# Stick-breaking and retention step: the places of the samples' pages, the last block of a group, and how the prompt's attention output is read

## The chip, the core and the metric

One NeuronCore of a Trainium2 chip runs the whole program. The metric is the device time of one execution in microseconds (us), and the time of a kernel is the median of its runs. The engines are TensorE (PE in the profile; PEld is its loading of weights), VectorE (DVE), ScalarE (ACT), GpSimd (POOL) and SyncE (SP). SP issues most DMAs, POOL issues the indirect ones. Each of them works through its own instructions in a fixed order.

## What is computed

One layer of a decoder, for a prompt of 1024 positions and for 8 samples of 8 new positions with 2048 past positions each. The part that matters here is stick-breaking attention, 8 heads of 64:

```python
def sb_block(q, k, v, q_pos, bias):
    z = jnp.einsum('bqhd,bkhd->bhqk', q, k) * (SB_HEAD_DIM ** -0.5)
    z = z + bias[None, :, None, None]
    mask = jnp.arange(k.shape[1])[None, :] < q_pos[:, None]
    log_stay = jnp.where(mask, jax.nn.log_sigmoid(-z), 0.0)
    tail = lax.cumsum(log_stay, axis=3, reverse=True) - log_stay
    a = jnp.where(mask, jnp.exp(jax.nn.log_sigmoid(z) + tail), 0.0)
    return jnp.einsum('bhqk,bkhd->bqhd', a, v)
...
    m = sigmoid(a_sb) * (o_sb @ w_sb_out) + sigmoid(a_r) * (o_r @ w_ret_out)
    h = h + rms_norm(m @ w_o, g_m_post)
```

The keys and values of a sample's past lie in 16 pages of 128 positions each, in a pool in HBM, in an order that a table gives; a page of keys is 256 KB for all heads, and the kernel reads 512 KB at once. Before and behind the mixer stand two SwiGLU layers that the change doesn't touch.

## The kernel before

`mixer_in` (L1471) makes the mixer's projections, retention, the prompt's attention (`prompt_sb`, L888) and the samples' attention (`decode_sb`, L1070); `mixer_out` (L1510) multiplies what attention gave with w_sb_out, adds the retention branch and multiplies with w_o. A framework arranges the instructions of each engine at compile time: it goes through the program in its order and simulated time and takes what is ready. Tiles lie in pools, pools are laid out as a stack, and a pool that is opened where older ones were closed lies on their bytes. On the chip an instruction waits only for earlier users of its own bytes.

**Fill.** Products that nobody waits for soon (gates and the retention branch's output, 448 steps of `gate_steps` and `ret_steps`) are given out as fill: `through(gen, k)` runs a generator and takes k fill steps for each of its yields. A step is some products of 320 or 384 columns on TensorE (L133, L137, L138). FILL_DEC has the five values of k for decode: one for the logits of group 0, one for each of the pairs (logits of group g + 1, values of group g), one for the values of group 3. 12 steps stand between the prompt's heads and decode. What is left of the fill runs behind decode.

**The prompt's heads.** Each of 8 heads has four tiles of 4 KB a partition, qs, kh, kl and vs, in the pool pqk, with three buffers each: heads 0, 3 and 6 share one, 1, 4 and 7 another, 2 and 5 the third. A head's block goes: two products into PSUM (L1031, L1032), sigmoids on ACT, a copy of the last column (L1047), a scan (L1049) and a product (L1050) on DVE, transposes on TensorE (L999), their high and low parts (L96 on ACT, L99 on DVE), products with vs (L1011), and the output through ost to osT in HBM (L1018, L1019).

**The samples.** Two samples make a group, there are four groups. `logits(g)` has 8 blocks of keys; for one it gathers two tiles of pages (L1100), transposes them in 16 products (L1202) into kt, with two copies each on DVE (L1207) and ACT (L1209), and with one block's lag multiplies kt with the queries qd (`product`, L1115). After every second block the sigmoids (L1149, L1150), the scan (L1156) and the product bt (L1157) follow, and with a further lag bt's transposes (`weights`, L1179, copied at L1180). The last block's product and weights stand at the end of `logits`, one behind the other (L1219 to L1224). `values(g)` gathers pages of values and multiplies them with the weights, from the last block to the first. `both` takes a step of logits and a step of values in turn. Key pages have six buffers and value pages five, in the pool decp, that lies on pqk; the first page tile lies on the qs of heads 0, 3 and 6. The query tile qd, the new keys kn and two kt are in deck; kn and qd lie on the vs of head 7, kt on what follows it. The bias rows brow (L1085, 16 small DMAs), the mask, the result odec and the weights of the new keys atn (L1109, a memset) are in dec, on the prompt's pt, bt and at.

**The end of decode.** The remaining fill runs, odec goes to the last 64 columns of osT (L1275), and `mixer_out` reads osT in three chunks of columns, four tiles each, into raw tiles sq (L1528) of the pool mg, that lies on the mixer's input u; from them come the high parts sh on ACT (L96) and the low parts sl on DVE (L99), in the pool mo, that lies on decode's pools. Products with w_sb_out follow (L1533 to L1548), for which SP loads the gates and the retention branch into the tiles xr (L1542, L1544) of mg.

Of the kernel before, what the change touches and what calls it, by code (L numbers as in the profile page):

```python
# [43 lines left out]
FILL_DEC = (.6, .8, .8, .8, .6)  # L44
# [24 lines left out]
class Trunk:  # L69
# [99 lines left out]
    def setup(self):  # L169
        nc, io = self.nc, self.io  # L170
        self.const = self.pool("const")
        self.wraw = self.pool("wraw")
        self.psum = self.pool("psum", space=PSUM)
        self.dram = self.pool("dram", space=DRAM)
        cp = self.const
        self.ident = self.t(cp, [P, P], "ident")
        make_identity(nc, self.ident)
        self.ones = self.t(cp, [P, P], "ones")
        nc.vector.memset(self.ones, 1.0)
        self.minus_half = self.t(cp, [P, 4], "mhalf")  # L180
        nc.gpsimd.memset(self.minus_half, -0.5)
        self.rowix = self.t(cp, [P, NB * PAGES // 2], "rowix", I32)
        self.gain = {}
        self.xT = self.t(self.dram, [D, T], "xT")
        self.h1T = self.t(self.dram, [D, T], "h1T")
        self.h2T = self.t(self.dram, [D, T], "h2T")
        self.osT = self.t(self.dram, [512, T], "osT")
        self.orT = self.t(self.dram, [D, T], "orT")
        self.gaT = self.t(self.dram, [D, T], "gaT")
        self.gbT = self.t(self.dram, [D, T], "gbT")  # L190
        self.grT = self.t(self.dram, [D, T], "grT")
        self.mrT = self.t(self.dram, [D, T], "mrT")
        self.unT = self.t(self.dram, [D, 512], "unT")
        self.cB = self.t(self.dram, [P, 8, 4, 288], "cB")
# [693 lines left out]
    def prompt_sb(self):  # L888
        nc, io = self.nc, self.io
        win = io["w_in"][0]  # L890
        with ExitStack() as ctx:
            qp = self.pool("pqk", ctx)
# [12 lines left out]
            def proj(p):  # L905

                qs = [self.t(qp, [P, TP], "qs", F32R, bufs=3) for e in range(2)]
                kh = [self.t(qp, [P, TP], "kh", F32R, bufs=3) for e in range(2)]
                kl = [self.t(qp, [P, TP], "kl", F32R, bufs=3) for e in range(2)]
                vs = [self.t(qp, [P, 8, P], "vs", F32R, bufs=3) for e in range(2)]  # L910
# [159 lines left out]
    def decode_sb(self):  # L1070
# [5 lines left out]
        with ExitStack() as ctx:  # L1076
            pp = self.pool("decp", ctx)
            kp_ = self.pool("deck", ctx)
            dp = self.pool("dec", ctx)
# [11 lines left out]
            kn = self.t(kp_, [P, 4, TD], "kn")  # L1091
# [13 lines left out]
            qd = self.t(kp_, [P, 288], "qd")  # L1105
            nc.gpsimd.memset(qd, 0.0)
# [17 lines left out]

            def logits(g, ats):


                qv = qd.rearrange("q (b x) -> q b x", x=144)[:, :, :P].rearrange("q b (m y) -> q b m y", y=32)
# [54 lines left out]
                def product(ps, b2, j, kt):  # L1183
                    side_by_side(ps, partial(query, b2), lambda m: kt[:, m, :], b2 == 0, b2 == 1)
                    if b2:
                        bt = self.t(dp, [P, 512], "bt", bufs=2)
                        left[0] = stick(bt, ps.rearrange("q (h i x) -> q h x i", h=2, i=2), 512, left[0])
                        todo.append((j, bt))

                late, todo, left = [], [], [None]  # L1190
                nk = new_keys()
                step = 0
                for j in range(NG - 1, -1, -1):
                    ps = self.bank("pb")
                    for b2 in range(2):
                        kp = [gather(self.t(pp, [P, 1024], "page", bufs=6), ck, 2 * g + b2, 2 * j + x)
                              for x in range(2)]
                        kt = self.t(kp_, [P, 4, 512], "kt", bufs=2)
                        for m in range(4):
# [10 lines left out]
                            if late and m == 1:  # L1210
                                product(*late.pop(0))
                            if todo and b2 == 1:
                                weights(*todo.pop(0))
# [4 lines left out]
                        late.append((ps, b2, j, kt))  # L1218
                while late:  # L1219
                    product(*late.pop(0))  # L1220
                yield
                while todo:
                    weights(*todo.pop(0))
                yield  # L1224

            def values(g, ats):
                po = self.bank("pm")
                for b2 in range(2):
                    out = po[:, b2 * P : (b2 + 1) * P]
                    for j in range(NG, -1, -1):  # L1230
                        for i in range(4 if j < NG else 1):
                            if j < NG and i % 2 == 0:
                                vp = gather(self.t(pp, [P, 1024], "vpage", bufs=5), cv, 2 * g + b2, 2 * j + i // 2)
# [32 lines left out]
            for g in range(4):  # L1266
                if g < 3:
                    new = {}
                    self.through(both(logits(g + 1, new), values(g, ats)), FILL_DEC[1 + g])
                    ats = new  # L1270
                else:
                    self.through(values(g, ats), FILL_DEC[4])
            while self.tiles or self.live:
                self.fill(1)
            nc.sync.dma_start(self.osT.rearrange("(m q) t -> q m t", q=P)[:, :, TP:T], ost)  # L1275
# [234 lines left out]
    def mixer_out(self):  # L1510
        nc, io = self.nc, self.io
        mch = [(0, 512), (512, 288), (800, 288)]
        with ExitStack() as ctx:
# [6 lines left out]
            with ExitStack() as ctx2:  # L1520
                op = self.pool("mo", ctx2)
                sh, sl = {}, {}
                for c, (o, n) in reversed(list(enumerate(mch))):
                    sh[c], sl[c] = (self.t(op, [P, 4, n], f"s{x}{c}", F32R) for x in "hl")
                for c, (o, n) in enumerate(mch):
                    for q in range(4):
                        raw = self.t(gp, [P, 512], "sq", bufs=4)
                        nc.sync.dma_start(raw[:, :n], self.osT[q * P : (q + 1) * P, o : o + n])  # L1528
                        self.hi(sh[c][:, q, :n], raw[:, :n])
                        self.lo(sl[c][:, q, :n], raw[:, :n], sh[c][:, q, :n])  # L1530
# [303 lines left out]
```

## Time and profile before

| | us |
|---|---|
| median of 3 runs | 2906.24 |
| the runs | 2904.14 to 2907.02 |
| the profiled execution, device time | 2907.92 |
| its span in the profile | 2906.2 |
| mean granted clock of TensorE, share of full speed | 0.986 |

The span is what the profiler recorded of one execution. Head 7 of the prompt ends at about 1658 us of it, decode runs from there to about 1952, and the products with w_sb_out follow. Times on the left of a timeline's rows are us from the start of the span. In a row of the stretches the length of the stretch is followed by the busy time of each engine with the number of its instructions. The granted clock is a share of 2.4 GHz, so that 0.50 is 1.2 GHz. "issue" as a releaser means that the engine waited for nothing that the profile shows.

### The profile page before, as it was taken

What the parts mean: (1) busy time and instruction counts of PE and PEld (TensorE: products, weight loads), DVE (VectorE), ACT (ScalarE), POOL (GpSimd) and SP (SyncE); (2) the same over time, 40 slices, a digit from 0 to 9 for tenths busy, and PEclk for the clock granted to TensorE, in tenths of its full rate; (3) what the DMA queues carried; (4) which work ended last, traced back from release to release, by engine and by line L of the source; (5) the groups of instructions that cost most, each with busy time, mean ns of one, the idle gap of its engine ahead of it and who ended that gap; (6) DMA issues with size and microseconds to landing.
All of it is one profiled execution on the core that took longest, in us unless ns stands there. A gap on an engine that the chain in (4) does not pass through costs nothing.

```text
span 2906.2 us, 51637 instructions
## 1 busy us (share of the span) xinstructions
PE 2804.2 (96%) x20064; PEld 2638.4 (91%) x20064; DVE 2033.5 (70%) x3962; ACT 1221.7 (42%) x2498; POOL 763.1 (26%) x687
## 2 busy tenths in 40 slices
PE   7999999999999999999999889989989999999998
PEld 6998899999999999989999767778988998999998
DVE  7878878888753543546888654436578888788776
ACT  5443444443343333335666542213344444434443
POOL 2334413333150000000000245520024335133321
PEclk8999999999999999999999999999999999999998
DMA  6544443333242322332222389876324335433431
GB/s 168 149 129 130 152 153 123 103 118 108 78 152 88 102 84 85 93 113 79 76 74 76 124 301 321 294 253 192 107 80 127 116 111 180 129 101 106 133 88 42
DMA packets 420420, 380.63 MB, mean 131 GB/s; under 512 B 30352, under 2 KB 380944, under 8 KB 420176
## 3 DMA queue, kind: packets, MB, share of 16 engines
q1 hardware_dynamic: 397904, 306.03, 34.4%
q0 software_dynamic: 22272, 71.31, 7.2%
q8 instruction: 157, 2.57, 0.4%
q14 instruction: 87, 0.71, 0.1%
HBM read 310.03 MB, written 63.05 MB: 128 GB/s over the span
## 4 chain that ended last, share of the span: by engine, by line
PE 59%; DVE 4%; issue 3%; DMA 1%; POOL 1%; ACT 1%; another core or an unknown queue 0%; SPq 0%; POOLq 0%; DVEq 0%; ACTq 0%
PE pa L133 11%; PE pa L138 10%; PE pa L137 10%; PE pb L133 3%; PE pb L138 3%; PE pb L137 3%; PE pc L133 3%; PE pc L137 3%; PE pc L138 3%; PE pc L1202 2%; PE pm L1115 1%; PE pm L1011 1%; PE pc L999 1%; PE pb L1115 1%; DVE sl L99 1%
## 5 line engine op out<-in xcount | busy, mean ns | idle before, releaser
L96 ACT ACTIVATE sh<-wr 128x512 fp32r<-128x512 f32 x592 | 339.2, 622 | 394.3 <-POOL wr L590 161.6
L133 PE MATMUL pa<-uh,wh 128*128 128x384 f32 (+1 forms) x1408 | 477.6, 339 | 4.7 <-ACT qdec L920 2.0
L138 PE MATMUL pa<-uh,wl 128*128 128x384 f32 (+1 forms) x1408 | 465.4, 331 | 0.0
L137 PE MATMUL pa<-ul,wh 128*128 128x384 f32 (+1 forms) x1408 | 464.3, 330 | 0.4 <-POOL ul L99 0.4
L133 PE MATMUL pa<-q,sh 128*128 128x256 f32 (+1 forms) x1408 | 411.7, 292 | 31.8 <-ACT hf L658 15.7
L99 DVE TENSOR_TENSOR sl<-wr,sh 128x512 fp32r<-128x512 f32 x592 | 397.0, 698 | 60.3 <-ACT sh L96 56.6
L137 PE MATMUL pa<-q,sh 128*128 128x256 f32 (+1 forms) x1408 | 409.6, 291 | 1.8 <-DVE q L99 1.8
L138 PE MATMUL pa<-q,sl 128*128 128x256 f32 (+1 forms) x1408 | 408.8, 290 | 0.8 <-DVE sl L99 0.8
L137 PE MATMUL pc<-hl,whd 128*128 128x256 f32 (+2 forms) x1088 | 350.2, 323 | 1.6 <-DVE hl L99 1.6
L138 PE MATMUL pc<-hh,wld 128*128 128x256 f32 (+2 forms) x1088 | 350.1, 323 | 0.0
L133 PE MATMUL pc<-hh,whd 128*128 128x256 f32 (+2 forms) x1088 | 343.4, 324 | 4.4 <-DVE y L718 2.4
L718 DVE TENSOR_TENSOR y<-y,pc 128x256 f32<-128x256 f32 (+2 forms) x496 | 248.8, 515 | 133.6 <-PE pc L138 131.3
L133 PE MATMUL pb<-q,sh 128*128 128x288 f32 (+1 forms) x1088 | 313.8, 289 | 3.3 <-ACT q L96 1.5
L138 PE MATMUL pb<-q,sl 128*128 128x288 f32 (+1 forms) x1088 | 314.5, 289 | 0.4 <-DVE sl L99 0.4
L137 PE MATMUL pb<-q,sh 128*128 128x288 f32 (+1 forms) x1088 | 314.7, 289 | 0.0
L133 PEld LDWEIGHTS pa<-q,sh 128*128 128x128 f32 x1408 | 268.5, 191 | 38.6 <-ACT hf L658 17.6
L133 PEld LDWEIGHTS pa<-uh,wh 128*128 128x128 f32 x1408 | 266.4, 189 | 20.8 <-issue 10.2
L137 PEld LDWEIGHTS pa<-q,sh 128*128 128x128 f32 x1408 | 268.3, 191 | 4.0 <-DVE q L99 2.1
L138 PEld LDWEIGHTS pa<-q,sl 128*128 128x128 f32 x1408 | 267.7, 190 | 2.1 <-DVE sl L99 1.0
L137 PEld LDWEIGHTS pa<-ul,wh 128*128 128x128 f32 x1408 | 266.4, 189 | 3.3 <-issue 1.4
L138 PEld LDWEIGHTS pa<-uh,wl 128*128 128x128 f32 x1408 | 265.8, 189 | 2.8 <-issue 1.7
L588 POOL TENSOR_TENSOR wr<-wr 128x512 f32<-128x512 f32 x78 | 125.7, 1612 | 481.8 <-DVE sl L99 476.7
(340 smaller groups left out, 5962.5 us busy)
## 6 DMA issues: line engine op xcount, KB each, us to landing
wr<-in_w_ffn_gu_dram SPq DMA_DIRECT2D x176, 512.0 KB
wrd<-in_w_ffn_down_dram SPq DMA_DIRECT2D x88, 512.0 KB
wr<-in_w_in_dram SPq DMA_DIRECT2D x56, 512.0 KB
q<-cB SPq DMA_DIRECT2D x16, 576.0 KB
wr<-in_w_o_dram SPq DMA_DIRECT2D x10, 512.0 KB
cB<-y SPq DMA_DIRECT2D x32, 144.0 KB
cB<-xr SPq DMA_DIRECT2D x32, 144.0 KB
s<-in_state_ret_dram SPq DMA_DIRECT2D x16, 256.0 KB
```

The lines of the kernel that those rows point to most:

```text
L96: return self.nc.scalar.activation(dst, src, AF.Copy)
L99: (eng or self.nc.vector).tensor_tensor(dst, src, hi.bitcast(F32), op=ALU.subtract)
L133: ins = mm(ps, wh, xh, start=first, stop=False)
L137: mm(ps, wh, xl, start=False, stop=False)
L138: mm(ps, wl, xh, start=False, stop=last)
L588: tt(v1, v0, v1, op=ALU.add)
L718: nc.vector.tensor_tensor(y[p][:, d, c], y[p][:, d, c], ps[:, :n], op=ALU.add)
L999: nc.tensor.transpose(tp[:, j * P : (j + 1) * P], bt[:, j * P : (j + 1) * P], self.ident)
L1011: ins = nc.tensor.matmul(po[:, lo:256], vs[:, j, :], ats[j // 4][x][:, j % 4, lo:256], start=(j == 0 and x == 0), stop=(j == last and x == 1))
L1115: return nc.tensor.matmul(out[32 * m : 32 * m + 32], w(m), x(m), start=first, stop=last, skip_group_check=True)
L1202: ins = nc.tensor.transpose(tp[:, i * P : (i + 1) * P], kp[i // 2][:, (i % 2) * 512 + m * P : (i % 2) * 512 + (m + 1) * P], self.ident)
```

## The change

The tiles of the prompt's heads are put into three pools, one for heads 0, 3, 6, one for 1, 4, 7, one for 2, 5. Decode opens a pool on each: dec0 holds four key pages, dec1 four value pages, dec2 the first kt, one key page, kn and now two tiles qd, one for the even and one for the odd groups. The rest (the second kt, one key page, one value page, the mask, brow, odec, atn and the working tiles) lies in dec. Pages and kt are taken in turn from lists, beginning with kp4, kp0 and kt0. The lists of what is still to do (`late`, `todo`) now outlive a group: the product and the weights of a group's last block are done inside the next group, and for group 3 by `last_block`, beside its values. FILL_DEC changes with it. The samples' result goes to a tensor of its own, osD. In `mixer_out` the rows are loaded straight into sl, two quarters at once, and the low part is made in place; the places of sh and sl change, chunk 0 lowest, on what was kt, kp4, kn and qd.

```diff
@@ -41,7 +41,7 @@
 GATES_FIRST = 4
 FILL_RET, FILL_SB = 40, 12
 FILL_HEADS = ((2, 4), (2, 4), (2, 4), (2, 2))
-FILL_DEC = (.6, .8, .8, .8, .6)
+FILL_DEC = (1., .8, .8, .7, .5)
 BEHIND = 12
 LAG_P = 2
 NEW_KEYS = (2, 6)
@@ -184,7 +184,8 @@
         self.xT = self.t(self.dram, [D, T], "xT")
         self.h1T = self.t(self.dram, [D, T], "h1T")
         self.h2T = self.t(self.dram, [D, T], "h2T")
-        self.osT = self.t(self.dram, [512, T], "osT")
+        self.osT = self.t(self.dram, [512, TP], "osT")
+        self.osD = self.t(self.dram, [512, TD], "osD")
         self.orT = self.t(self.dram, [D, T], "orT")
         self.gaT = self.t(self.dram, [D, T], "gaT")
         self.gbT = self.t(self.dram, [D, T], "gbT")
@@ -889,7 +890,7 @@
         nc, io = self.nc, self.io
         win = io["w_in"][0]
         with ExitStack() as ctx:
-            qp = self.pool("pqk", ctx)
+            places = [self.pool(f"pqk{i}", ctx) for i in range(3)]
             sp = self.pool("pst", ctx)
             bp = self.pool("pbeta", ctx)
             ap_ = self.pool("pat", ctx)
@@ -904,10 +905,11 @@
 
             def proj(p):
 
-                qs = [self.t(qp, [P, TP], "qs", F32R, bufs=3) for e in range(2)]
-                kh = [self.t(qp, [P, TP], "kh", F32R, bufs=3) for e in range(2)]
-                kl = [self.t(qp, [P, TP], "kl", F32R, bufs=3) for e in range(2)]
-                vs = [self.t(qp, [P, 8, P], "vs", F32R, bufs=3) for e in range(2)]
+                at = [places[(2 * p + e) % 3] for e in range(2)]
+                qs = [self.t(x, [P, TP], "qs", F32R) for x in at]
+                kh = [self.t(x, [P, TP], "kh", F32R) for x in at]
+                kl = [self.t(x, [P, TP], "kl", F32R) for x in at]
+                vs = [self.t(x, [P, 8, P], "vs", F32R) for x in at]
                 for e in range(2):
                     heads[2 * p + e] = qs[e], kh[e], kl[e], vs[e]
 
@@ -1074,9 +1076,19 @@
         NG = PAGES // 4
         PAST = PAGES * PAGE
         with ExitStack() as ctx:
-            pp = self.pool("decp", ctx)
-            kp_ = self.pool("deck", ctx)
-            dp = self.pool("dec", ctx)
+
+            p0, p1, p2, dp = (self.pool(x, ctx) for x in ("dec0", "dec1", "dec2", "dec"))
+            key_pages = [(p2, "kp4")] + [(p0, f"kp{i}") for i in range(4)] + [(dp, "kp5")]
+            value_pages = [(p1, f"vp{i}") for i in range(4)] + [(dp, "vp4")]
+            key_parts = [(p2, "kt0"), (dp, "kt1")]
+            for pl, tag, n in ((p2, "kt0", 2048), (p2, "kp4", 1024), (dp, "kt1", 2048), (dp, "kp5", 1024),
+                               (dp, "vp4", 1024)):
+                self.t(pl, [P, n], tag)
+
+            def in_turn(places, shape):
+                places.append(places.pop(0))
+                return self.t(places[-1][0], shape, places[-1][1])
+
             mask = self.t(dp, [P, 4, TD], "dmask")
             nc.sync.dma_start(mask, io["c_decmask"])
 
@@ -1088,7 +1100,7 @@
             nc.vector.tensor_scalar(brown, brow, -1.0, None, op0=ALU.mult)
             ost = self.t(dp, [P, 4, TD], "odec")
 
-            kn = self.t(kp_, [P, 4, TD], "kn")
+            kn = self.t(p2, [P, 4, TD], "kn")
             tp = self.bank("pc")
             for m in range(4):
                 nc.tensor.transpose(tp[:, m * TD : (m + 1) * TD], self.knew[:64, m * P : (m + 1) * P],
@@ -1102,8 +1114,9 @@
                 return t
 
 
-            qd = self.t(kp_, [P, 288], "qd")
-            nc.gpsimd.memset(qd, 0.0)
+            qds = [self.t(p2, [P, 288], f"qd{x}") for x in range(2)]
+            for x in range(2):
+                nc.gpsimd.memset(qds[x], 0.0)
             atns = [self.t(dp, [P, P], f"atn{x}") for x in range(2)]
             for x in range(2):
                 nc.gpsimd.memset(atns[x][64:128], 0.0)
@@ -1122,9 +1135,12 @@
                         self.behind(ins, before.ins)
                 return ins
 
+            late, todo = [], []
+
             def logits(g, ats):
 
 
+                qd = qds[g % 2]
                 qv = qd.rearrange("q (b x) -> q b x", x=144)[:, :, :P].rearrange("q b (m y) -> q b m y", y=32)
                 for e in range(2):
                     ln = slice(64 * e, 64 * e + 64)
@@ -1185,17 +1201,17 @@
                     if b2:
                         bt = self.t(dp, [P, 512], "bt", bufs=2)
                         left[0] = stick(bt, ps.rearrange("q (h i x) -> q h x i", h=2, i=2), 512, left[0])
-                        todo.append((j, bt))
-
-                late, todo, left = [], [], [None]
+                        todo.append(partial(weights, j, bt))
+
+                left = [None]
                 nk = new_keys()
                 step = 0
                 for j in range(NG - 1, -1, -1):
                     ps = self.bank("pb")
                     for b2 in range(2):
-                        kp = [gather(self.t(pp, [P, 1024], "page", bufs=6), ck, 2 * g + b2, 2 * j + x)
+                        kp = [gather(in_turn(key_pages, [P, 1024]), ck, 2 * g + b2, 2 * j + x)
                               for x in range(2)]
-                        kt = self.t(kp_, [P, 4, 512], "kt", bufs=2)
+                        kt = in_turn(key_parts, [P, 4, 512])
                         for m in range(4):
                             tp = self.bank("pc")
                             for i in range(4):
@@ -1208,19 +1224,20 @@
                             else:
                                 nc.scalar.activation(kt[:, m, :], tp, AF.Copy)
                             if late and m == 1:
-                                product(*late.pop(0))
+                                late.pop(0)()
                             if todo and b2 == 1:
-                                weights(*todo.pop(0))
+                                todo.pop(0)()
                             step += 1
                             if step in NEW_KEYS:
                                 next(nk, None)
                             yield
-                        late.append((ps, b2, j, kt))
-                while late:
-                    product(*late.pop(0))
-                yield
-                while todo:
-                    weights(*todo.pop(0))
+                        late.append(partial(product, ps, b2, j, kt))
+
+            def last_block():
+                late.pop(0)()
+                for _ in range(4):
+                    yield
+                todo.pop(0)()
                 yield
 
             def values(g, ats):
@@ -1230,7 +1247,7 @@
                     for j in range(NG, -1, -1):
                         for i in range(4 if j < NG else 1):
                             if j < NG and i % 2 == 0:
-                                vp = gather(self.t(pp, [P, 1024], "vpage", bufs=5), cv, 2 * g + b2, 2 * j + i // 2)
+                                vp = gather(in_turn(value_pages, [P, 1024]), cv, 2 * g + b2, 2 * j + i // 2)
                             src = vp[:, (i % 2) * 512 : (i % 2 + 1) * 512] if j < NG else self.vnew
                             a = ats[j][:, i, :] if j < NG else ats[j]
                             ins = side_by_side(out, lambda m: a[:, 32 * m : 32 * m + 32],
@@ -1269,10 +1286,10 @@
                     self.through(both(logits(g + 1, new), values(g, ats)), FILL_DEC[1 + g])
                     ats = new
                 else:
-                    self.through(values(g, ats), FILL_DEC[4])
+                    self.through(both(last_block(), values(g, ats)), FILL_DEC[4])
             while self.tiles or self.live:
                 self.fill(1)
-            nc.sync.dma_start(self.osT.rearrange("(m q) t -> q m t", q=P)[:, :, TP:T], ost)
+            nc.sync.dma_start(self.osD.rearrange("(m q) t -> q m t", q=P), ost)
 
     def retention(self):
         nc, io = self.nc, self.io
@@ -1520,14 +1537,19 @@
             with ExitStack() as ctx2:
                 op = self.pool("mo", ctx2)
                 sh, sl = {}, {}
-                for c, (o, n) in reversed(list(enumerate(mch))):
+                for c, (o, n) in enumerate(mch):
                     sh[c], sl[c] = (self.t(op, [P, 4, n], f"s{x}{c}", F32R) for x in "hl")
                 for c, (o, n) in enumerate(mch):
+                    lf = sl[c].bitcast(F32)
+                    m = min(n, TP - o)
+                    for q in range(0, 4, 2):
+                        qq = slice(q * P, (q + 2) * P)
+                        nc.sync.dma_start(lf[:, q : q + 2, :m], self.osT[qq, o : o + m].rearrange("(k p) t -> p k t", p=P))
+                        if m < n:
+                            nc.sync.dma_start(lf[:, q : q + 2, m:], self.osD[qq, :].rearrange("(k p) t -> p k t", p=P))
                     for q in range(4):
-                        raw = self.t(gp, [P, 512], "sq", bufs=4)
-                        nc.sync.dma_start(raw[:, :n], self.osT[q * P : (q + 1) * P, o : o + n])
-                        self.hi(sh[c][:, q, :n], raw[:, :n])
-                        self.lo(sl[c][:, q, :n], raw[:, :n], sh[c][:, q, :n])
+                        self.hi(sh[c][:, q, :], lf[:, q, :])
+                        self.lo(sl[c][:, q, :], lf[:, q, :], sh[c][:, q, :])
                 w1 = [self.unit(io["w_sb_out"][0][:, j * 256 : (j + 1) * 256].rearrange("(k p) c -> p k c", p=P))
                       for j in range(4)]
                 for c, (o, n) in enumerate(mch):
```

## Rows read from the trace of the kernel before

**Rows 1.** The page, part 1: busy time of each engine, its share, instructions.
```profile
PE 2804.2 (96%) x20064; PEld 2638.4 (91%) x20064; DVE 2033.5 (70%) x3962; ACT 1221.7 (42%) x2498; POOL 763.1 (26%) x687
```

**Rows 2.** Busy time by stretch: PE, PEld, DVE, ACT, POOL; granted clock, DMA share, GB/s.
```profile
1636.00:1649.00 13.00, 6.84 (x39) 5.02 (x39) 12.00 (x24) 6.68 (x13) 0.56 (x3) 0.85 0.09 24
...
1660.00:1670.00 10.00, 7.13 (x49) 5.49 (x48) 0.69 (x1) 2.65 (x9) 5.45 (x6) 0.83 0.79 312
...
1709.00:1716.00 7.00, 1.59 (x36) 0.64 (x28) 2.42 (x4) 2.75 (x7) 3.52 (x4) 0.82 0.94 327
...
1780.00:1790.00 10.00, 7.78 (x114) 6.59 (x108) 4.26 (x14) 1.51 (x3) 4.14 (x4) 1.00 0.79 279
...
1850.00:1917.00 67.00, 67.00 (x708) 50.02 (x711) 29.74 (x48) 18.18 (x30) 29.41 (x28) 1.00 0.78 263
1917.00:1941.00 24.00, 23.88 (x292) 19.20 (x281) 4.78 (x10) 1.24 (x2) 9.16 (x10) 1.00 0.89 323
...
1950.00:1958.00 8.00, 0.48 (x1) 0.48 (x2) 3.55 (x6) 1.65 (x3) 0.00 (x0) 0.65 0.70 236
```

**Rows 3.** The same view: the stretches right behind three of the gaps.
```profile
1645.00:1653.00 8.00, 6.35 (x29) 5.49 (x30) 3.74 (x7) 1.19 (x2) 3.65 (x6) 0.57 0.34 103
1664.00:1670.00 6.00, 4.71 (x36) 3.89 (x37) 0.69 (x1) 2.14 (x7) 1.93 (x4) 0.72 0.63 244
1716.00:1720.00 4.00, 3.90 (x17) 3.93 (x18) 3.12 (x6) 1.21 (x3) 0.00 (x0) 0.50 1.04 412
```

**Rows 4.** Timeline of PE: start, us, instruction; last value products of head 6.
```profile
1623.44 1.88 PE L1011 MATMUL pm<-at,vs 128*128 128x256 f32 x15
```

**Rows 5.** Timeline of POOL, idle time before and its releaser in brackets.
```profile
1621.50 2.70 POOL L99 TENSOR_TENSOR wl<-wr,wh 128x1024 fp32r<-128x1024 f32 x1 [49.96 <-ACT wh L96]
1647.67 0.34 POOL L1109 MEMSET atn<- 64x128 f32 x2 [23.46 <-DVE bt L1050]
1648.78 1.06 POOL L1100 DMA_INDIRECT page<-in_cache_k_dram,rowix  x1 [0.77 <-issue]
...
1664.63 0.34 POOL L1106 MEMSET qd<- 128x288 f32 x1
```

**Rows 6.** Timeline of SP's queue at the end of head 7.
```profile
1658.15 0.45 SPq L1019 DMA_DIRECT2D osT<-ost  x1
...
1660.68 8.29 SPq L1085 DMA_DIRECT2D brow<-in_sb_bias_dram  x14
```

**Rows 7.** Decode's page gathers and key copies: count, duration ns min/median/max, first and last start.
```profile
L1100 POOL DMA_INDIRECT page<-in_cache_k_dram,rowix x64: 932/939/1696, 1648.8 to 1887.7; - x64
...
L1209 ACT ACTIVATE kt<-pc x64: 577/598/612, 1665.4 to 1908.4; 128x512 f32<-128x512 f32 x64
L1207 DVE COPY kt<-pc x64: 658/690/693, 1665.4 to 1911.4; 128x512 f32<-128x512 f32 x64
```

**Rows 8.** Timelines of PE, ACT and DVE at the end of group 0.
```profile
1708.13 0.60 PE L1202 MATMUL pc<-ident,page 128*128 128x128 f32 x4
...
1709.55 1.04 PE L1115 MATMUL pb<-kt,qd 128*32 128x512 f32 x8
1716.10 1.09 PE L1179 MATMUL pc<-ident,bt 128*128 128x128 f32 x4 [5.51 <-DVE bt L1157]
...
1713.21 0.69 ACT L1149 ACTIVATE pt<-pb,brown 128x512 f32<-128x512 f32 x1 [4.39 <-remote]
...
1715.26 0.69 DVE L1157 TENSOR_TENSOR bt<-bt,pt 128x512 f32<-128x512 f32 x1
```

**Rows 9.** Timelines of SP's queue and of PE at the end of decode.
```profile
1951.66 0.52 SPq L1275 DMA_DIRECT2D osT<-odec  x1
1952.53 0.33 SPq L1528 DMA_DIRECT2D sq<-osT  x1
...
1954.90 0.45 SPq L1542 DMA_DIRECT2D xr<-gaT  x1
...
1957.52 1.22 PE L133 MATMUL pa<-sh,wh 128*128 128x512 f32 x2 [7.66 <-ACT sh L96]
```

## The prediction

> **What bounds the kernel now.** I read the page first, then busy time and clock stretch by stretch around the samples' attention, then the order of work on POOL, SP and PE at the places where TensorE stops. [rows 1] is the page: TensorE is busy 96% of the span, DVE 70%. So the change pays only where TensorE stops or runs at 1.2 GHz. The stretches of [rows 2] show where: it is busy 6.84 of 13 us in the tail of head 7, where DVE is busy 12.00 of 13; 7.13 of 10 at 1660 to 1670, when the first pages come in; 1.59 of 7 at 1709 to 1716, the end of group 0; 7.78 of 10 at 1780 to 1790, the end of group 1; and 0.48 of 8 at 1950 to 1958, between decode and the output products. Group 3 (1850 to 1917) has no gap. After the long gaps the granted clock stands at about half [rows 3]. Of busy time b at granted clock c, b(1-c) would be saved at 2.4 GHz: 6.35 x 0.43 = 2.7 us, 4.71 x 0.28 = 1.3 us, 3.90 x 0.50 = 2.0 us. After the short gap in 1780 to 1790 the clock stays 1.00. Gaps and clock together: 6.2 + 2.9 + 5.4 + 2.2 + 7.5 and 6.0, so some 30 us, the whole of what can be won but for the clock behind the last gap.
>
> **What orders the start.** First gathers are not late because their bytes are taken. The first page tile lies on the q rows of heads 0, 3 and 6; head 6's last products with its values start at 1623.44 and run 1.88 us [rows 4]; the page is gathered at 1648.78, behind the atn memsets that waited 23.46 us for the last block of head 7 [rows 5]. The qd memset stands at 1664.63, behind the write of head 7's output that SP issued at 1658.15 [rows 5, 6], though its own bytes are the values of head 7. I read this as a rule of the order made at compile time: what lies in a pool is placed behind the close of every pool beneath it, while the waits on the chip go tile by tile. Three pools for the heads then matter for the order.
>
> **Part 1, pages earlier.** dec0 lies on the pool of heads 0, 3, 6, dec2 on that of heads 2, 5, so kp4 can go when head 5 is through, kp0 to kp3 at about 1625, each at 0.939 us on POOL [rows 7]. That is five pages over 20 us earlier; kp5, vp4, kt1, atn and brow stay in the last pool, dec, which opens after head 7's output write. Of block 1 the 16 transposes (four take 0.60 us, so 2.4), its product (eight take 1.04 us [rows 8], so half) and nothing more can go into the 6.16 idle us of the tail, since block 2's keys need kt1: 2.9 us at most. Against that stand two kt copies of 0.690 us on a full DVE [rows 7]: 1.4 us of a longer tail; ACT's two of 0.598 us have room. Net 1.5. At 1660 to 1670 the 2.87 idle us and 1.3 us of clock are waits for pages, kn and kt; with five pages there I take 3.0 of these 4.2. Together 4.5 us. Bounds: -1.4 (only the copies) and 6.16 + 2.87 + 2.7 + 1.3 = 13.0 (every gap gone). I stay in the lower half, since kt1 opens no earlier. The brow loads, 14 in 8.29 us on SP from 1660.68 [rows 6], now stand behind the same output write; they land at 1670 to 1675. Nothing on TensorE needs them before the third PSUM bank of logits, four blocks on, so I cost that at nothing; without that cover it is up to 5 us. The second qd memset (0.34 us on POOL) and its ACT copies are hidden: POOL idles 23.46 us there [rows 5].
>
> The gathers now run beside a busy DVE. Of 64 page gathers the longest took 1.696 us where the median was 0.939 [rows 7]; five at that price are 8.5 us instead of 4.7, still over by about 1634, before block 1 could start. The Trainium skill, SBUF — State Buffer, section "SBUF: two separate sides" (the "DVE blocks DMA" trap), says that a transfer issued by GpSimd can't get its descriptors written while DVE holds the port they share, and gives some 3100 ns beside a copy where 620 ns are usual. By that figure five would be an estimated 15.5 us and the tail's 1.5 us would be lost: 2898 instead of 2896.5. This trace's 1.696 us sides with a smaller price.
>
> **Part 2, a group's last logits go into the next group.** At the end of group 0 TensorE issues the last product at 1709.55 and has nothing until 1716.10: sigmoids from 1713.21, the scan behind them, the product bt at 1715.26, then the transposes [rows 8]. The carry puts the product at the second step of the next group and the transposes some steps later, with transposes of pages, value products and fill between. A step there holds a quarter block of transposes (0.60), value products and 0.8 fill; the chain is 6.5 us and five or six steps cover it. So 5.51 us of wait and 2.0 us of clock go; I take 7.0. The 2.22 us at group 1's end are of the same kind; I take 1.5. Group 2's end shows no gap: nothing. In the last group values alone cover the chain, some 13 value steps and half as many fills: nothing lost, and up to 2 us if not. Bounds for this part: 4 (the chain half covered) and 9.7 (all).
>
> **Part 3, fill moved.** The fill is as long as before: 34 x 0.6 + 69 x 0.8 x 3 + 35 x 0.6 is 207 steps, after it 32 x 1.0 + 67 x (0.8 + 0.8 + 0.7) + 40 x 0.5 is 206. DMA moved 263 GB/s in group 3 and 323 in the last stretch [rows 2]; 0.7 instead of 0.8 makes group 3 some 3 us shorter, thus 275 GB/s, below the 323. Cost nothing; small new waits from the different mixing (TensorE's order, PSUM banks, SP) I put at 1.5 us, between 0 and 6.
>
> **Part 4, the output products.** SP issues the samples' write at 1951.66, the first load of the prompt's rows at 1952.53, and TensorE waits 7.66 us, till 1957.52, for ACT's first part of it [rows 9]. The prompt's rows need no samples, so one could hope for all 7.66 us. But raw rows now go into sl, in pool mo, that lies on dec and dec2; by the rule above its loads stand behind the close of dec, which is the end of the samples' write. The xr loads lie in another pool, that opens with the last fill, and were issued from 1954.90 behind four sq loads; now they can go first. Of these, 256 KB each, four or five fit into the write's time; SP issues one in about 0.5 us, and five are 1.28 MB, 3.1 us at the 412 GB/s of [rows 3]. The first sl load is 512 KB instead of 256, 0.6 us more. Against the four sq loads it replaces that makes TensorE start about 1.8 us later: a loss of 1.8, with bounds of 5 lost and, if the loads do go early, 7.66 + 1 won. Fewer, larger loads save SP some 2 us that nobody waits for.
>
> **Sum.** 4.5 + 7.0 + 1.5 - 1.5 - 1.8 = 9.7 us. The profiled execution took 2907.92 us (span 2906.2), 1.7 above the median 2906.24. The same change on the median gives **2896.5 us**, with a range of its own from 2890 to 2902.
>
> **Rivals.**
> The loads go early (2887): the rows of the prompt are placed before the last values, as sl0 lies on kt and kp4, idle by then. For it: the waits on the chip go by tiles, and the write has a tensor of its own. Against it: the order seen on POOL [rows 5]. Then part 4 gives 7.7 instead of -1.8. Chance 0.2.
> Pages no earlier (2901): POOL still runs the atn memset before the first gather, or wl of a fill unit holds the queue. For it: that is the order now [rows 5]. Part 1 is then nothing. Chance 0.2.
> The change doesn't do what it says (2905): the carried block's transposes sit too early in TensorE's order and wait as before, and the start is as above. Chance 0.08.
> Slower (2915): transposes of block 1 are placed in TensorE's order inside head 7's tail, at about 1637, and their page comes late, since POOL works in order and a wl ahead of the gather waits for a fill unit's weights. TensorE then stands before head 7's own transposes, and DVE's chain behind it. With a page as late as now, gathered at 1648.78, this costs 12 us, and 2 of clock; parts 2 to 4 give back 5.2. It is slower than no change by over 0.2% when the page is over 9 us late. For it: nothing in the queue lets a gather pass a wait. Against it: the wl at 1621.50 is through before [rows 5]. Chance 0.07.
> The main case has the rest, 0.45.
>
> **Numbers.** 0.2%, 5.8 us, is about what a measurement can tell from no change. Faster takes five sixths of the main case, all of the first rival and half of the second: 0.68. Same: the rest of these and the third, 0.24. Slower: 0.08. The range takes the main case, the early loads and the late pages with their bounds: 2884 to 2905.
>
> **What would show it.** Gathers from before 1630, five of them ahead of the atn memsets; TensorE's wait for bt of L1157 gone, its clock 1.00 at the end of group 0; the tail of head 7 busier by some 3 us; xr loads ahead of the sl loads and a wait for sh of some 9 us, not 7.66. I am wrong if sl is loaded before the last values are done, if the first gather still follows the memset, or if group 3 shows gaps.

## The result: no gain, and a quarter of a percent lost in the first set of runs

The median of the changed kernel is 2912.53 us in 20 runs, of before 2904.07 in 20 of the same set: ratio 1.0025, interval 1.0015 to 1.0034. Predicted were 2896.5 us, a ratio of 0.9967 to the 2906.24 then known. In a later set the ratio was 1.0006 (0.9994 to 1.0017). The kernel before had medians of 2904.07, 2903.92, 2910.34, 2912.11 and 2911.41 us in five sets; the second and third were taken on one chip. An interval covers the runs of one set and not this difference, so a ratio within some 0.3% of 1 is not safe by itself.

The first row is the page's busy time after, for [rows 1]; the next four are busy time by stretch, the columns those of [rows 2].

```profile
PE 2811.0 (97%) x20064; PEld 2638.4 (91%) x20064; DVE 2030.9 (70%) x3962; ACT 1220.8 (42%) x2498; POOL 762.3 (26%) x688
```
```profile
1636.00:1649.00 13.00, 8.58 (x56) 7.13 (x54) 12.77 (x30) 9.52 (x19) 3.10 (x3) 1.00 0.47 155
1649.00:1660.00 11.00, 8.62 (x46) 7.99 (x47) 4.12 (x7) 2.67 (x5) 0.00 (x0) 0.69 0.14 53
1660.00:1670.00 10.00, 10.00 (x82) 9.60 (x81) 1.81 (x4) 2.48 (x5) 5.66 (x7) 1.00 0.33 97
...
1709.00:1720.00 11.00, 7.55 (x45) 5.88 (x46) 6.88 (x10) 5.22 (x11) 5.01 (x3) 0.84 0.81 279
```

TensorE is busy 6.8 us longer for the same 20064 products. The gap at 1660 to 1670 is gone; in that at the end of group 0 it is busy 7.55 of 11 us, with the clock at 0.84 on average. POOL's timeline and SP's and PE's at the end of decode, for [rows 5, 9]:

```profile
1598.64 1.04 POOL L1112 DMA_INDIRECT kp<-in_cache_k_dram,rowix  x1 [0.23 <-PE pb L1034]
...
1627.74 1.44 POOL L1112 DMA_INDIRECT kp<-in_cache_k_dram,rowix  x1 [0.16 <-issue]
...
1664.85 0.34 POOL L1122 MEMSET atn<- 64x128 f32 x2
```
```profile
1950.89 0.37 SPq L1292 DMA_DIRECT2D osD<-odec  x1
...
1954.64 0.52 SPq L1564 DMA_DIRECT2D xr<-gaT  x1
...
1956.15 2.51 SPq L1547 DMA_DIRECT2D sl<-osT  x5
```
```profile
1962.48 1.22 PE L133 MATMUL pa<-sh,wh 128*128 128x512 f32 x2 [10.14 <-ACT sh L96]
```

Five pages of keys come before the atn memset, the first at 1598.64 and the last at 1632.03, and four of values. The sl loads are issued 5.26 us behind the samples' write, behind an xr load, and TensorE waits 10.14 us instead of 7.66 (7.7 to 9.2 in three profiles of before).

**A yardstick.** Up to head 5 both programs have the same order, and one execution differs from the next by some us there. So I count from the start of the last copy into knew (1571.4 before, 1574.7 after) to the end of fill, where TensorE's last wait begins. The row of that stretch, before, then after:

```profile
1571.40:1949.86 378.46, 359.17 (x3226) 287.94 (x3224) 192.61 (x369) 137.60 (x278) 148.15 (x140) 0.98 0.72 246
```
```profile
1574.70:1952.34 377.64, 363.30 (x3226) 285.49 (x3224) 190.10 (x371) 136.82 (x277) 148.48 (x141) 0.99 0.72 247
```

Idle time is the first number less the second. What the clock takes is the sum of b(1-c) over windows of 2 us. Busy time less that is **work**: what TensorE would be busy at 2.4 GHz. "Changes" counts in TensorE's compiled order of decode how often its products change between fill, transposes, products with keys and products with values.

| kernel | ratio, interval | changes | work | idle | clock | last wait | to the end |
|---|---|---|---|---|---|---|---|
| before, 3 profiles | 1 | 329 | 352.7 to 353.1 | 19.0 to 19.9 | 6.1 to 8.6 | 7.7 to 9.2 | 1334.8 to 1337.4 |
| changed, 3 profiles | 1.0025, 1.0006 | 394 | 359.0 to 359.3 | 14.0 to 14.5 | 4.3 to 4.4 | 10.1 to 10.3 | 1335.9 to 1337.0 |
| out_sq | 1.0022 (1.0011, 1.0032) | 394 | 358.9 | 16.5 | 7.3 | 8.2 | 1339.6 |
| nocarry | 1.0010 (1.0000, 1.0019) | 308 | 348.0 | 17.3 | 4.3 | 11.6 | 1330.3 |
| pools | 1.0010 (1.0001, 1.0019) | 318 | 349.2 | 18.5 | 7.9 | 7.5 | 1330.5 |
| carry | 1.0022 (1.0012, 1.0032) | 369 | 357.3 | 22.7 | 7.9 | 4.0 | 1342.1 |
| fb2 | 1.0003 (0.9994, 1.0012) | 327 | 353.5 | 21.9 | 7.7 | 5.9 | 1337.5 |
| **fb3** | **0.9957 (0.9945, 0.9970)** | 277 | 351.0 | 16.8 | 5.5 | 5.0 | 1326.6 |
| b_fb2 | 1.0021 (1.0011, 1.0031) | 285 | 350.4 | 22.1 | 8.1 | 8.9 | 1338.2 |
| fb3_nocarry | 1.0058 (1.0046, 1.0071) | 291 | 353.4 | 30.2 | 11.0 | 12.5 | 1356.3 |
| b_fb3 | 1.0050 (1.0037, 1.0063) | 258 | 352.0 | 31.8 | 10.9 | 6.4 | 1350.7 |
| fb3_sq | 0.9964 (0.9951, 0.9977) | 277 | 351.2 | 16.0 | 4.5 | 4.2 | 1328.1 |
| carry_fb3 | 0.9993 (0.9981, 1.0005) | 304 | 353.7 | 20.2 | 6.5 | 6.3 | 1336.2 |
| fb4 | 0.9984 (0.9973, 0.9996) | 263 | 348.7 | 22.8 | 12.2 | 6.7 | 1341.6 |

Work comes back within 0.4 us when the same order runs again; idle and clock time come back less well. out_sq has the changed kernel's 394 changes and its work, and yet 2 us more idle time and 3 more of clock, so 3 to 5 us of these two in a single profile decide nothing. The ratios of out_sq, nocarry, pools and carry are to a before of 2903.92 us, those from fb2 on to one of 2910.3 to 2912.1. By three profiles of each, the change bought 5 us of idle time and some 3 of clock with 6.3 us more work and 2.0 more of the last wait: nothing is left.

**Where the work comes from.** PE's timeline of the changed kernel, start and duration:

```profile
1704.82 1.09 PE L1218 MATMUL pc<-ident,kp 128*128 128x128 f32 x8
1705.67 0.39 PE L133 MATMUL pa<-uh,wh 128*128 128x320 f32 x1
1705.91 0.30 PE L137 MATMUL pa<-ul,wh 128*128 128x320 f32 x1
1706.05 0.31 PE L138 MATMUL pa<-uh,wl 128*128 128x320 f32 x1
...
1706.49 0.31 PE L138 MATMUL pa<-uh,wl 128*128 128x320 f32 x1
1706.73 0.43 PE L1128 MATMUL pm<-vp,at 128*32 128x128 f32 x8
```

Fill behind fill starts after 0.14 us; the fill behind transposes holds its successor 0.24 us, and the one ahead of value products 0.24. No such tenth shows as a wait. Over 1720 to 1940 the medians are the same in both kernels: 0.08 to 0.09 us more behind transposes, 0.09 ahead of values, 0.10 behind them. The change has 18 more steps from fill to values, 16 more back, 8 more from transposes to fill: 18 x 0.09 + 16 x 0.10 + 8 x 0.085 = 3.9 of the 6.3 us.

The order can be priced more fully: every product of the stretch by its kind and shape and by the kinds ahead of it and behind it (a wait counts as a kind), at its mean in the profiles of the other orders. For each of the 12 orders here that comes within 1.8 us of the work measured, with 353.9 to 354.3 us for before and 359.6 to 359.9 for the changed kernel: some 5.6 of the 6.3 us. So the order makes the work, but for the rest. The bare number of changes is a poor measure of it: b_fb3 has 71 fewer than before and 0.9 us less work, nocarry 86 fewer than the changed kernel and 11.2 less.

### The profile page after: what moved, and what is told of

Same layout as the page of the kernel before. It is cut to its first block, busy times and chain, and to the rows that moved or that the text cites. A ratio compares the mean times of both kernels' runs of the same rounds, so it can differ in the third digit from the quotient of the medians.

```text
span 2910.6 us, 51640 instructions
## 1 busy us (share of the span) xinstructions
PE 2811.0 (97%) x20064; PEld 2638.4 (91%) x20064; DVE 2030.9 (70%) x3962; ACT 1220.8 (42%) x2498; POOL 762.3 (26%) x688
```

## The experiments

"A" below is the theory that these changes of kind ate what the change won.

**Which part loses.** out_sq has the change with the old loads:

```diff
-                    lf = sl[c].bitcast(F32)
...
+                        raw = self.t(gp, [P, 512], "sq", bufs=4)
+                        nc.sync.dma_start(raw[:, :m], self.osT[q * P : (q + 1) * P, o : o + m])
+                        if m < n:
+                            nc.sync.dma_start(raw[:, m:n], self.osD[q * P : (q + 1) * P, :])
```

> The changed kernel with the loads ahead of w_sb_out as before (raw rows into sq, in a pool that opens with the last fill; the samples' rows from osD). In the profile of the changed kernel TensorE waits 10.1 us there against 7.7. Theory A (most of the loss is TensorE changing more often between fill, transposes of pages, products with keys and products with values: 394 changes in decode against 329; the loads cost 2.5 us): the wait comes back to 7.7 us, the time is 2.5 us under the changed kernel, ratio to before about 1.0016. Theory B (the loads make the whole loss): the ratio is 1.000 or less.

The last wait fell by 2 us, the time hardly: 1.0022. The loads are not the whole loss, as B had it.

nocarry flushes a group's last block inside its own logits:

```diff
                         late.append(partial(product, ps, b2, j, kt))
+                while late:
+                    late.pop(0)()
+                yield
+                while todo:
+                    todo.pop(0)()
+                yield
```

> The changed kernel, but a group's last product and weights stand at the end of its own logits as before; TensorE's order then has 308 changes of kind in decode. Theory A (each change costs some 0.06 us): the gap at the end of group 0 comes back (5 to 8 us), 86 changes fewer give 5.5 us back, so the time is about that of the changed kernel or up to 3 us under it, ratio 1.000 to 1.002, and TensorE is busy some 5 us less in decode. Theory C (changes of kind are free, the carry is worth its 7 us): 5 to 8 us slower than the changed kernel, ratio 1.005.

11 us less work than the changed kernel, and 1.0010: the ratio where A put it, though work fell by twice what A priced, and the time by 5.6 us, more than the 3 that A allowed. The wait at the end of group 0 came back with 2.96 us, not 5 to 8. So with fill step by step it is the carry that loses in the changed kernel: 11.2 us of work for 3 of idle time. Shorter waits of 1.54, 1.07 and 1.39 us in group 0, for keys and weights, stand here too, without the carry.

pools is nocarry and out_sq together with FILL_DEC as before: the new places alone.

> The kernel before with the three pools of heads and the places of the pages alone; fill shares, last blocks and the loads ahead of w_sb_out as before. 318 changes of kind. Theory A: the first pages come over 20 us early, TensorE's idle time in 1636 to 1670 goes from 9 to some 6 us and the clock there rises; 3 to 5 us faster than before, ratio 0.9985. Theory D (the early pages lengthen head 7's tail and win nothing): ratio 1.000 or above.

By its ratio of 1.0010 D has it. From the new keys to the end pools took 1330.5 us, though, 4 to 7 less than three profiles of before, which is A's 3 to 5; against the before of the later sets its 2906.85 us would be 0.998 to 0.999. Which of the two holds stays open. Work fell by 3.7 us, idle time over the whole stretch by 1 only. At 1636 to 1670 TensorE's idle time went from 9.1 to 6.8 us, nearly to A's 6, but a wait of 3.11 us for the weights of the new keys came in at 1672, and the one at the end of group 0 grew to 6.45. The early pages can't help in head 7's tail, as TensorE's order puts the first transposes of a page behind its last block:

```profile
1653.64 1.11 PE L1218 MATMUL pc<-ident,kp 128*128 128x128 f32 x4
```

(PE's timeline of the changed kernel; in before the first stands at 1661.45.)

carry is the kernel before with the carry alone (and osD for the samples' result):

```diff
-            qd = self.t(kp_, [P, 288], "qd")
+            qds = [self.t(kp_, [P, 288], f"qd{x}") for x in range(2)]
...
-                while late:
-                    product(*late.pop(0))
...
+            def last_block():
```

> The kernel before with the last block of a group done in the next group, alone; pools, fill shares and loads as before. 369 changes of kind against 329. Theory A: the gaps at the ends of groups 0 and 1 go (some 8 us with the clock), 40 more changes cost 2.6 us; 3 to 6 us faster, ratio 0.998 to 0.999. Theory E (the carry itself is what loses, by new waits of TensorE for keys and weights): ratio 1.001 or above.

A expected a gain: 1.0022. Work rose by 4.4 us, and idle time by 3 though the wait of 5.51 us was gone. E has the sign. Of the new waits the longest is not for keys or weights, as E had it, but one of the fill for VectorE to take up an earlier fill's product, which in turn waited for a load (PE's timeline of carry):

```profile
1756.14 0.63 PE L133 MATMUL pa<-uh,wh 128*128 128x320 f32 x1 [6.83 <-DVE gs L874]
```

It stands in one profile, of the slowest of nine runs, and in none of the changed kernel. Another, of 2.78 us, is for the memset of the second qd.

**Fewer changes, all else kept.** fb2 and fb3 give the same fill in twos and threes (up to two steps a group are left to run behind decode):

```diff
-            while due >= 1.0:
-                due -= 1.0
-                if other is None or next(other, self) is self:
+            while due >= (1.0 if other is not None else step):
+                due -= 1.0 if other is not None else step
+                if other is None:
+                    self.fill(int(step))
+                elif next(other, self) is self:
                     self.fill(1)
```

> The changed kernel with decode's fill given out two steps at a time instead of one; everything else of the change stays, the number of steps too. 327 changes of kind in TensorE's order instead of 394. By the timelines a fill product behind transposes starts its successor 0.085 us later than one behind fill, one ahead of value products 0.09, one behind them 0.10. Theory A (these changes ate what the carry won): TensorE is busy some 5 us less in decode than in the changed kernel, and the time is 4 to 6 us under it, ratio to before 1.000 to 1.001. Theory F (the loss comes from the waits for keys and weights that the carry makes): pairs of steps do not help, ratio 1.0025 or above.

> The changed kernel with decode's fill given out three steps at a time. 277 changes of kind. Theory A: by the same prices 8.8 us under the changed kernel unless longer stretches of fill delay the chain of logits; ratio to before 0.9985 to 1.000. Theory F: no gain, or a loss, since keys and weights wait behind longer fill; ratio 1.0025 or above.

fb2 stands at 1.0003, in A's range, but its 2913.16 us are not under the changed kernel's 2912.53 and 2914.24, where A had 4 to 6 us: 5.7 us less work went with 7.6 more of idle time and 3.3 of clock. fb3 stands at 0.9957, 11 us under before and 13 to 15 under the changed kernel, beyond what A priced. The stretch of fb3, columns as above, has 7 us less busy time than the changed kernel:

```profile
1573.60:1946.85 373.25, 356.50 (x3226) 289.86 (x3225) 184.85 (x371) 136.63 (x276) 148.06 (x141) 0.98 0.73 249
```

To the end of the span fb3 is 10 us shorter than the changed kernel. Of that 8 are work, and 5 are the last wait, which no change of kind explains; idle time and clock give 4 back.

b_fb2 gives the kernel before fill by twos:

> The kernel before with decode's fill given out two steps at a time, nothing else. 285 changes of kind instead of 329. Theory A: by the prices of the timelines 3.1 us less, ratio 0.9985 to 0.9995. Theory F: no difference, 1.000 or above.

Its work fell by 2.5 us, where A had 3.1, but idle time rose by 3: 1.0021. Fewer changes alone do not make a kernel faster.

> The kernel before once more, for a second profile: the same order of instructions, so what differs from the first profile is what one execution differs from another. The first profile lies 3.8 us above the median of 29 runs. From the last new keys of the prompt (start of the last copy into knew) to the end of the span it took 1334.8 us; if the profiles of the other kernels are to be read by that stretch, this one should take 1331 to 1335 us.

It took 1337.4 us, outside the 1331 to 1335 expected, with work of 352.9: the stretch to the end is good to some 3 us.

**What fill by three needs.** fb3_nocarry is fb3 with nocarry's edit, b_fb3 the kernel before with step 3.

> The changed kernel with fill three steps at a time and without the carry: a group's last product and weights stand at the end of its own logits. 291 changes of kind against 277 with the carry. Theory A (the carry wins its 7 us where it brings no more changes of kind): the gap at the end of group 0 is back and the time lies 4 to 9 us above fill by three with the carry, ratio to before 0.997 to 0.999. Theory E (the carry itself loses): it lies below fill by three with the carry, ratio under 0.9955.

> The kernel before with decode's fill three steps at a time, nothing else. 258 changes of kind against 329. By pairs the same kernel lost 0.2%, with TensorE 2.6 us less busy at full clock and 2 to 3 us more idle. Theory A: by the prices of the timelines 6.6 us less work, so 3 to 6 us faster unless idle time eats it as with pairs, ratio 0.998 to 1.000. Theory G (fewer changes help only together with the early pages and the carry, which fill the gaps that longer stretches of fill leave): ratio 1.001 or above.

1.0058 and 1.0050. The carry is worth 1% here, three times what A had. b_fb3's work fell by 0.9 us where A priced 6.6. PE's timeline of fb3_nocarry at its end of group 0:

```profile
1727.28 1.10 PE L1197 MATMUL pc<-ident,bt 128*128 128x128 f32 x4 [6.83 <-DVE bt L1175]
```

Idle time is 30.2 us instead of fb3's 16.8 and the clock takes twice as much. G is borne out for the carry.

> The changed kernel with fill three steps at a time and the loads ahead of w_sb_out as before (sq). In the profile with the new loads TensorE waits only 5.0 us there, since fill ends 3 us after the samples' result. Theory A (the loads cost some 2 us, as the pools beneath them close last): wait 3 to 4 us, ratio 0.995 to 0.9957. Theory H (the new loads are as good): ratio 0.9957 or above.

0.9964, not to be told from 0.9957; the wait fell to 4.2, and 2.5 us for an xr load came behind it. The two loads are as good here.

> The changed kernel once more, for a second profile. What the order of instructions sets should come back within 0.5 us: TensorE's busy time less what the clock takes, 359.0 us from the last new keys to the end of fill in the first profile (353.0 in both of before). Idle time and clock may differ by some us.

Work 359.3, idle 14.0: the order's part repeats.

**What was still open** was whether the change loses at all, and what makes fb3's gain.

> The changed kernel again, timed. If the loss lies in the program, the ratio to before is again 1.0015 to 1.0034. If the first figure was a matter of that chip, or of how the runs fell, it is 0.9985 to 1.001, as the profiles' stretch from the last new keys on (1335.9 and 1336.7 us against 1334.8 and 1337.4) has it.

1.0006: neither clearly the first figure nor clearly none. Medians of the changed kernel were 2912.5 and 2914.2; those of before moved from 2904 to 2910 and above, with the same program. What before does in its faster sets no profile of mine shows, so a loss of 0 to 0.3% stays with its last part unexplained.

> The kernel before with the carry and with fill three steps at a time, but its own pools and places of the pages, fill shares and loads. 304 changes of kind. If the carry makes the gain by closing the gaps that longer fill leaves: ratio 0.996 to 0.998, since the early pages are worth 1 to 3 us. If the early pages make it: ratio 1.002 or above, near the 1.005 of fill by three alone.

0.9993, between the two expectations: the carry takes back the 0.5% of fill by three, and new places, loads and fill shares make the rest, 0.36%, with 27 fewer changes. They were not parted further.

> The changed kernel with fill four steps at a time. 263 changes of kind against 277 by three. Theory A: 1.2 us less work; if the chain of logits is not kept waiting, ratio 0.995 to 0.996; if longer fill starts to delay keys and weights, as without the carry, 0.997 or above.

0.9984: work fell by 2.3 us, but idle time rose by 6 and the clock took 6.7 more. Three is the best of 1 to 4.

> The kernel before, for a third profile: TensorE's work at full clock from the last new keys to the end of fill again 353 us within 0.5, and 1331 to 1338 us from the last new keys to the end.

Work 352.7, 1337.2 us to the end.

## Why the prediction was wrong

**Part 3, the step that failed.** "Small new waits from the different mixing" I put at 1.5 us, at most 6. It was some 11. As waits it was 5.0 to 5.3 us in group 0 (PE's timeline of the changed kernel):

```profile
1703.01 0.66 PE L1218 MATMUL pc<-ident,kp 128*128 128x128 f32 x4 [1.21 <-DVE at L1196]
...
1709.82 0.65 PE L1218 MATMUL pc<-ident,kp 128*128 128x128 f32 x4 [1.22 <-ACT kt L1225]
...
1714.95 1.56 PE L1128 MATMUL pb<-kt,qd 128*32 128x512 f32 x8 [2.63 <-DVE kt L1223]
```

They stand in nocarry and not in pools, which has the old fill shares and loads; as the loads come 230 us later, I lay these waits to the larger share of fill in group 0, which no run changes alone. The other 6.3 us are work that shows as no wait. Taken by edits, the new places took 3.7 us of work off (pools), shares and loads 1.2 more (nocarry), and the carry put 11.2 on. I had a bound of 6 and the rows of decode with their starts, and did not count the changes of a finer mixing.

**Parts 1 and 2 together.** Idle time fell by 5 us and the clock's share by 3. Without the new waits in group 0 that makes 13, the 13.0 that I had. For Part 1 that is partly luck.

**Part 1.** The order of POOL and the rule of pools held: five pages of keys at 1598 to 1632, then the atn memset. The tail grew by 1.1 us (1.4 priced). But I put block 1's work into the tail; TensorE's order did not, and its waits for blocks of the last heads (from 1590 on) rose from 6.1 to 7.4 us. The 2.9 us at 1660 to 1670 went, with the low clock there; the other stretch at half clock only moved, to 1651 to 1657. Of the five pages four cost 1.44, 0.99, 0.95 and 0.93 us, at 1627 to 1633, where DVE is busy 5.76 of 6 us with scans and products. The 3.1 us that the Trainium skill gives beside a copy (SBUF — State Buffer, "SBUF: two separate sides", the "DVE blocks DMA" trap) do not show here.

**Part 2.** The wait of 5.51 us went, as did the 2.22 at the end of group 1. But I expected a clock of 1.00 at the end of group 0: behind the new waits it stood at 0.50 for some 3 us in each of three profiles.

**Part 4.** Mechanism and size were right: the loads stand behind the close of dec, 2.0 us lost for 1.8. I let four or five xr loads go first; it was one, and SP had waited 3 us for a weight load's place.

By the first ratio the rival "slower" (2915, a ratio of 1.003) came nearest, by the second "doesn't do what it says" (2905, 0.9996). The mechanism of neither happened: the transposes of the carried block did not wait as before, and the pages came early, not late. Both of my ranges, to 2902 and to 2905, end below the medians of 2912.5 and 2914.2.

## What to carry to other kernels

Where a bound engine interleaves several kinds of product, look at which kind stands next to which in its order: a step from fill to values or back cost some 0.1 us here as plain busy time, and what a profile calls idle can be bought at that price. The mere count of such steps did not tell the work. Group the cover work first, then move latencies under it: fill by three lost 0.5% alone and, with the carried block and the early pages, won 0.4%. And an order made at compile time goes by pools even where the waits on the chip go by tiles.

## What was not expected of the hardware

The longest of the new waits for keys, 2.63 us, is a collision. DVE's timeline, then POOL's, in the changed kernel:

```profile
1711.65 2.67 DVE L1172 TENSOR_TENSOR_SCAN pt<-pt 128x513 f32<-128x513 f32 x1 [1.12 <-ACT pt L1165]
1714.23 0.66 DVE L1223 COPY kt<-pc 128x512 f32<-128x512 f32 x1
```
```profile
1710.86 2.37 POOL L99 TENSOR_TENSOR wl<-wr,wh 128x1024 fp32r<-128x1024 f32 x1 [2.26 <-ACT wh L96]
```

The scan's median is 1.23 us; begun while POOL subtracts, it ends 1.1 us behind POOL's end and holds kt's copy. It took 2.67 us in all three profiles. The Trainium skill (SBUF — State Buffer, "SBUF: two separate sides") has it that the two share a port that one holds for a whole instruction; these rows agree, as the 1.1 us are nearly a scan's 1.23. In fb3 no scan took over 1.23 us.

Behind the same short gaps at 1272 to 1284, with the same instructions, the granted clock stayed at 1.00 in one profile of before and fell to 0.50 at 1284 to 1286 in another.
